# Another order of the eight head pairs in an encoder layer on one core, with two weight scans moved to other pairs

## The chip, the cores and the metric

One core of a Trainium2 chip. The metric is device time in microseconds (us) of one execution, and shorter is better. Five engines work side by side, each through its own queue in order: PE (matrix products), DVE (vector), ACT (activation functions), POOL and SP; SP here only issues transfers, the transposing ones among them. All dependencies between engines are semaphores.

## The reference, cut to what matters

One pre-norm layer over 2048 positions of width 1024. Eight heads of width 64 attend within a band of nine chunks of 64 positions (kind A); four heads of differential attention attend to everything up to the own chunk (kind B, two maps of width 64 for each head). Then an output projection, a gated FFN with a causal convolution, and norms.

```python
h = rmsnorm(x, attn_norm_g)
qa, ka, va, qb, kb, vb = jnp.split(h @ w_in, 6, axis=-1)
oa = chunked_band_attention(qa, ka, va, a_rel_bias)
ob = diff_attention(qb, kb, vb, t5_bias, lam, subln_g, lam_init)
x = x + jnp.concatenate([oa, ob], axis=-1) @ w_out
h = rmsnorm(x, ffn_norm_g)
u = causal_dwconv(h @ w_up, conv_w, conv_b)
gate, val = jnp.split(u, 2, axis=-1)
x = x + (jax.nn.silu(gate) * val) @ w_down
return rmsnorm(x, final_norm_g)
```

## The kernel before, in words

All products are made of float16 halves (a value is a high and a low part, three products of the four are added up). The attention works through eight head pairs, two heads of kind A (pairs 0 to 3) or the two maps of one kind B head (pairs 4 to 7), in the order of the list `ORDER` (L436). A place is a position in that list: place 1 is n = 0 in the code, place 8 is n = 7. Each pair has 16 blocks of 128 query rows.

For a block, `front_a` or `front_b` makes the scores on PE (L434, two PSUM banks for each piece of up to 512 keys), adds the bias and takes the maximum on DVE (L478 for A, L537 for B), forms the exponent's offset (L483, L541), takes the exponential on ACT (L486, L544), for B subtracts the second map from the first on DVE (L560; on ACT and POOL for some, L557 and L558), splits the result into halves (ACT L487 or L562, DVE and POOL L488, POOL L563) and has SP transpose it into the tile `pt` (L489, L565). Two blocks later `back_a` or `back_b` multiplies with the values (L509, L583). A block of kind A has rows of at most 640 keys, a block of kind B of up to 2048: A is the short kind, B the long one. Kind B goes through its blocks as 0, 15, 1, 14 and so on, kind A in order.

Between these steps, PE gets filler: `units(n)` lists the projections (L375) of the next pair's K, V and first Q, and of this pair's other Q, as generators; one pull is 6 products with 512 columns or 12 with 256. A pair takes 48 pulls, spread evenly over its 16 blocks, place 7 takes 32 and place 8 takes 28 over its first 11 blocks; after that place 8 pulls from the first output projection, `out_proj(0)` (L654). `beside(n)` holds what else is done at a block of a pair: the fetch of a weight slice and its row sums of squares (`scan_w`), its scaling and splitting (`load_w`, POOL and ACT), the bias of the next pair (`load_bias`). Two entries stand at place 7: `scan_wo` fetches w_out in eight pieces into two buffers (`wraw`) and squares them on ACT (L606), `scan_wd` fetches two pieces of w_down and takes their maxima on DVE (L614). Both results are needed only at place 8 or in the FFN.

Attention steps carry a high priority, and the framework's scheduler fixes each engine's order when the program is built; so the lists above set what can be chosen, and the printed order of each engine tells what came of it. Before the first pair, `make_profiles_b` writes the T5 profiles (31 small copies, L308) and `make_profiles` the band profiles, each to DRAM, from which `load_bias` reads rows. The FFN (L859 on) and the down product (L1258) follow in an order written out by hand.

Of the kernel before, what the change touches and what calls it, by code (L numbers as in the profile page):

```python
# [33 lines left out]
NH2 = 8  # L34
# [33 lines left out]
def kernel(  # L68
# [137 lines left out]
    with ExitStack() as at:  # L206
# [87 lines left out]
        def make_profiles():  # L294

            rr = sb.tile([8, 257], F32, name="rr", tag="PT", bufs=3)
            nc.gpsimd.dma_start(rr, rel_rev)
            pa = sb.tile([8, PROF], F32, name="pa", tag="HL", bufs=2)
            V.tensor_copy(pa[:, 0:127], rr[:, 0:1].to_broadcast([8, 127]))
            V.tensor_copy(pa[:, 127:PROF], rr[:, 0:256])  # L300
            nc.gpsimd.dma_start(prof[0:8], pa)

        def make_profiles_b():
            t5 = sb.tile([8, 32], F32, name="t5", tag="PT", bufs=3)
            nc.gpsimd.dma_start(t5, t5_t)
            pb = sb.tile([8, PROF], F32, name="pb", tag="HL", bufs=2)
            for j0, j1, k in T5_RUNS:
                V.tensor_copy(pb[:, j0:j1], t5[:, k:k + 1].to_broadcast([8, j1 - j0]))  # L308
            nc.gpsimd.dma_start(prof[8:16], pb)
# [123 lines left out]
                for hd, (a, b) in enumerate(((0, 64), (64, 128))):  # L433
                    nc.tensor.matmul(ps[hd], lhsT=qs[a:b, qa, qc], rhs=ks[a:b, ka, kc], start=n == 0, stop=n == 2)  # L434

        ORDER = [4, 5, 0, 6, 1, 7, 2, 3]  # L436
        oTl = {}

        def store_oT(c, tg, osb):
# [3 lines left out]
            V.tensor_tensor(hl[:, 1], src, hl[:, 0], ALU.subtract)  # L443
            last = c == ORDER[-1]
            st = kv.tile([P, 2, 4, P], F16, name="ost_l", tag="vs") if last else \
                sb.tile([P, 2, 4, P], F16, name="ost", bufs=1)
            nc.sync.dma_start_transpose(st.rearrange("p a t q -> p (a t) q"), hl.rearrange("p a b -> p (a b)"))
            if last:
                oTl[tg] = st
                return  # L450
            nc.sync.dma_start(oTd[tg, :, :, ORDER.index(c)], st)

# [181 lines left out]
        def out_proj(pc):  # L634


            for t in range(4):
                ss = tiny.tile([P, 2], F32, name="ss2")
                xs = []
                for sd in range(2):  # L640
# [9 lines left out]
                    for n in range(2):  # L650
                        k = 0
                        for c, oc in enumerate(lhs):
                            for a, b in TERMS:
                                nc.tensor.matmul(ps[n], lhsT=oc[:, a], rhs=wo[ORDER[c]][:, b, n * TG:(n + 1) * TG],  # L654
                                                 start=k == 0, stop=k == 3 * NC - 1)
# [51 lines left out]
        for tg in range(NG):  # L707
            make_h(tg, xts if tg == 0 else None)
            if tg == 0:
                for k, j in enumerate((2, 1, 0)):  # L710
                    scan_w(w, ORDER[0], j, raws[k] if k < len(raws) else None)
                    load_w(w, j, (True, KF, Q1)[k])
            proj_v_first(w, tg)
            run(proj_k(w, tg))
            if tg == 0:
                run(proj_q(w, 0))
                make_lambda()
                make_profiles_b()
                load_bias(w, ORDER[0])
        run(proj_q(w, 1))  # L720
        make_profiles()

        ws = [w] + [weights(n) for n in range(1, NH2)]
        first = out_proj(0)
# [16 lines left out]
        def beside(n):  # L741

            todo = {}
            if n == 0:
                todo[0, 0] = lambda: scan_w(ws[1], ORDER[1], 1)
                todo[0, 1] = lambda: load_w(ws[1], 1)
            if n + 1 < NH2:
                x = ws[n + 1]
                todo[3, 0] = lambda: scan_w(x, ORDER[n + 1], 2)
                todo[4, 1] = lambda: load_w(x, 2)  # L750
                todo[7, 0] = lambda: scan_w(x, ORDER[n + 1], 0)
                todo[8, 1] = lambda: (load_w(x, 0), load_bias(x, ORDER[n + 1]))
            if n + 2 < NH2:
                todo[13, 0] = lambda: scan_w(ws[n + 2], ORDER[n + 2], 1)
                todo[14, 1] = lambda: load_w(ws[n + 2], 1)
            if n == NH2 - 2:
                todo[10, 0] = scan_wo
                todo[13, 0] = scan_wd
            if n == NH2 - 1:
                todo[8, 1] = load_wo  # L760
            return todo
# [592 lines left out]
```

## Time and profile before

| | us |
|---|---|
| median of 3 runs | 2524.24 (2523.07 to 2527.94) |
| the profiled execution | 2528.28 |
| its span, first to last instruction | 2526.5 |
| busy PE / DVE / ACT / POOL in the span | 2379.4 / 1846.0 / 1354.3 / 1164.6 |
| first score product of place 1 | 79.5 |
| first score product of places 2 to 8 | 228.2, 376.6, 488.8, 640.8, 747.7, 896.8, 994.5 |
| first FFN product | 1273.6 |

The span holds a first part (norms, transposes and the first pair's projections), the attention, the output projection and the FFN. The starts of the places come from counting the score products (L434) in PE's order and taking the time of the first one of each pair from the trace. A stretch below is the time from one such start to the next one, and carries the number of its place. Granted clock 1.00 means that TensorE had its upper level (2.4 GHz) all through a stretch; 0.5 is the lower one (1.2 GHz).

### The profile page before, as it was taken

To read this page: it belongs to the slowest core of one execution; us is meant where nothing else is said; L and a number is where in the kernel's file an instruction comes from. 1 tells how busy PE (TensorE), PEld (TensorE's weight loads), DVE (VectorE), ACT (ScalarE), POOL (GpSimd) and SP (SyncE) were. 2 spreads that over 40 slices of the span, in tenths; PEclk is the share of its full clock that TensorE was granted. 3 is DMA by queue.
4 is the path that set the end of the run, shared out by engine and by line. 5 is a ranking of instruction groups with operands and counts; after the bars stand their busy time and mean duration, and the time that the engine had idled before them with its cause. 6 is when DMAs were issued, how large, how long until landed. Compare 5 with 4: busy or idle time off the path is not lost.

```text
span 2526.5 us, 42303 instructions
## 1 busy us (share of the span) xinstructions
PE 2379.4 (94%) x15382; PEld 1219.7 (48%) x15382; DVE 1846.0 (73%) x4359; ACT 1354.3 (54%) x2399; POOL 1164.6 (46%) x1127
## 2 busy tenths in 40 slices
PE   6999899999899988997978999999999999999998
PEld 5655555555565555543433444444444444444443
DVE  8678787568757885766566888888888776656555
ACT  7566566456655666644335666566556553333322
POOL 3343443234323332224234665666566464766654
PEclk9999899999999999998999999999999999999999
DMA  6154457635673579895995324333333339323322
GB/s 192 29 101 88 94 104 139 121 73 96 134 143 73 100 128 226 162 242 167 277 225 154 123 96 129 106 121 97 123 112 111 105 111 398 101 88 113 109 88 80
DMA packets 625378, 333.34 MB, mean 132 GB/s; under 512 B 447864, under 2 KB 592528, under 8 KB 623760
## 3 DMA queue, kind: packets, MB, share of 16 engines
q1 hardware_dynamic: 615264, 316.15, 50.2%
q0 software_dynamic: 2432, 8.42, 0.9%
q10 hardware_dynamic: 7472, 6.06, 0.8%
q8 instruction: 120, 1.97, 0.3%
q14 instruction: 90, 0.74, 0.1%
HBM read 145.73 MB, written 82.08 MB: 90 GB/s over the span
## 4 chain that ended last, share of the span: by engine, by line
PE 36%; DVE 6%; DMA 3%; ACT 3%; issue 2%; POOL 2%; SPq 1%; ACTq 0%; DVEq 0%; POOLq 0%
PE mm L859 21%; PE mm L1258 13%; DMA wd<-gd 2%; DVE Y L1058 1%; SPq L1093 1%; PE omm L654 1%; DVE wdhl L889 1%; ACT wuraw L959 1%; DMA T<-td 1%; DMA wdraw<-in_w_down_dram 0%; DMA wd<-wdd 0%; ACT Y L1062 0%; ACT wdhl L886 0%; DVE hl L681 0%; POOL wuhl L977 0%
## 5 line engine op out<-in xcount | busy, mean ns | idle before, releaser
L859 PE MATMUL mm<-T,wuhl 128*128 128x512 f16 x3696 | 809.0, 381 | 18.2 <-ACT tmp L1030 14.9
L859 PEld LDWEIGHTS <-wuhl 128*128 128x128 f16 x3696 | 363.4, 99 | 456.2 <-issue 25.5
L1258 PE MATMUL mm<-wd,ghl 128*128 128x512 f16 x1848 | 401.9, 380 | 4.7 <-ACT ghl L133 3.5
L375 PEld LDWEIGHTS <-whl 128*128 128x128 f16 x2976 | 273.1, 99 | 233.6 <-issue 81.4
L375 PE MATMUL mm<-h,whl 128*128 128x512 f16 x1440 | 349.2, 385 | 0.0
L434 PE MATMUL s<-ks,qs 64*128 64x256 f16 (+3 forms) x2160 | 282.1, 295 | 29.0 <-DVE mx L478 14.4
L1258 PEld LDWEIGHTS <-ghl 128*128 128x128 f16 x1848 | 180.7, 98 | 225.2 <-ACT ghl L133 4.8
L563 POOL TENSOR_TENSOR phl<-St,phl 128x1024 f16<-128x1024 f32 (+7 forms) x96 | 155.7, 1633 | 248.8 <-ACT phl L562 233.7
L1058 DVE SCALAR_TENSOR_TENSOR Y<-U,taps,Y 128x1024 f32<-128x1024 f32 x176 | 256.9, 1460 | 6.2 <-ACT Y L1054 4.6
L544 ACT ACTIVATE St<-St,nb,sc 128x1024 f32<-128x1024 f32 (+4 forms) x192 | 187.9, 979 | 50.3 <-DVE nb L541 50.3
L133 ACT ACTIVATE ghl<-wd,gsc 128x384 f16<-128x384 f32 (+1 forms) x176 | 106.6, 660 | 196.6 <-DMA wd<-gd 92.1
L134 DVE SCALAR_TENSOR_TENSOR ghl<-wd,gsc,ghl 128x384 f16<-128x384 f32 (+1 forms) x176 | 137.0, 812 | 94.3 <-ACT ghl L133 94.0
L375 PE MATMUL mq<-h,whl 128*128 128x256 f16 x1536 | 205.0, 278 | 0.0
L488 POOL TENSOR_TENSOR phl<-St,phl 128x640 f16<-128x640 f32 (+2 forms) x64 | 80.9, 1264 | 255.0 <-ACT phl L487 246.3
L434 PEld LDWEIGHTS <-qs 64*128 64x128 f16 x2160 | 114.4, 96 | 152.5 <-issue 108.0
L537 DVE CUSTOM_DVE_ANT_0 St<-s,near,mxb 128x512 f32<-128x512 f32 (+2 forms) x280 | 166.7, 620 | 25.5 <-PE s L434 19.8
L654 PE MATMUL omm<-wohl,oT 128*128 128x512 f16 x672 | 155.6, 386 | 18.5 <-DVE x L660 18.5
L889 DVE SCALAR_TENSOR_TENSOR wdhl<-wdraw,wd_sc,wdhl 128x128 f16<-128x128 f32 x132 | 141.5, 1087 | 30.8 <-ACT wdhl L886 29.7
L968 POOL TENSOR_TENSOR Sx<-wuraw 128x512 f32<-128x512 f32 x44 | 77.4, 1760 | 163.2 <-ACT wuraw L959 156.0
L1062 ACT ACTIVATE Y<-Y 128x1024 f32<-128x1024 f32 x44 | 46.5, 1057 | 182.2 <-DVE Y L1058 182.2
L486 ACT ACTIVATE St<-St,nb,sc 128x640 f32<-128x640 f32 (+4 forms) x128 | 107.9, 843 | 59.3 <-DVE nb L483 58.1
L562 ACT ACTIVATE phl<-St 128x1024 f16<-128x1024 f32 (+7 forms) x96 | 75.6, 802 | 114.1 <-DMA pt<-phl 56.6
(229 smaller groups left out, 3765.9 us busy)
## 6 DMA issues: line engine op xcount, KB each, us to landing
wd<-gd SPq DMA_DIRECT2D x88, 256.0 KB, 2.8
wuraw<-in_w_up_dram SPq DMA_DIRECT2D x42, 512.0 KB, 5.2
gd<-Y SPq DMA_DIRECT2D x42, 512.0 KB, 2.8
wdraw<-in_w_down_dram SPq DMA_DIRECT2D x154, 128.0 KB, 2.8
wd<-wdd SPq DMA_DIRECT2D x11, 1792.0 KB, 13.1
wdd<-wdhl SPq DMA_DIRECT2D x41, 448.0 KB, 2.7
wraw<-in_w_in_dram SPq DMA_DIRECT2D x24, 512.0 KB, 3.9
td<-hl SPq DMA_DIRECT2D x24, 512.0 KB, 5.0
```

Of the source, the lines that this page charges most:

```text
L134: V.scalar_tensor_tensor(lo, src, scale, hi, ALU.mult, ALU.subtract)
L375: nc.tensor.matmul(ps, lhsT=hl[:, a, c, :], rhs=h[:, b, c, t0:t1], start=n == 0, stop=n == 3 * NC - 1)
L434: nc.tensor.matmul(ps[hd], lhsT=qs[a:b, qa, qc], rhs=ks[a:b, ka, kc], start=n == 0, stop=n == 2)
L486: A.activation(St, St, AF.Exp, bias=nb[:, hd:hd + 1], scale=w["sc"], accum_out=l[:, hd:hd + 1])
L537: V.tensor_tensor_reduce(Sm[hd][g][:, a0:a0 + b - a], ps[hd][:, :b - a], bias, 1.0, m[hd], ALU.add, ALU.max, mx[:, hd, f:f + 1])
L544: A.activation(Sm[hd][g], Sm[hd][g], AF.Exp, bias=nb[:, hd:hd + 1], scale=w["sc"], accum_out=l[:, hd, g:g + 1])
L563: nc.gpsimd.tensor_tensor(hl[:, 1], Sm[0][g], hl[:, 0], ALU.subtract)
L654: nc.tensor.matmul(ps[n], lhsT=oc[:, a], rhs=wo[ORDER[c]][:, b, n * TG:(n + 1) * TG], start=k == 0, stop=k == 3 * NC - 1)
L859: nc.tensor.matmul(ps, lhsT=hl[:, a, wop, c * P:(c + 1) * P], rhs=Tt[:, b, c, :], start=start and k == 0, stop=k == 11, skip_group_check=n ...
L889: V.scalar_tensor_tensor(dst, src, scale, h, ALU.mult, ALU.subtract)
L1058: V.scalar_tensor_tensor(Y, self.U[j][:, tap:D + tap], self.u.taps[j][:, tap:tap + 1], Y, ALU.mult, ALU.add)
L1258: nc.tensor.matmul(ps[m].rearrange("p (c n) -> p c n", c=4), lhsT=g[kb][:, a, go], rhs=wd[kb][:, :, c_, wo_], start=kb == k0 and k == 0, s ...
```

## The change

The list of pairs becomes 0, 4, 1, 5, 2, 6, 7, 3. In letters, before B B A B A B A A, now A B A B A B B A. Place 8 keeps pair 3. Since a pair of kind A comes first, its profiles are written ahead of the T5 ones. `scan_wo` moves from place 7 to place 4 (a pair of kind B), `scan_wd` from place 7 to place 6 (also B). The pulls stay with the places: 48, and 32 and 28 at the last two.

```diff
--- before.py
+++ after.py
@@ -433,7 +433,7 @@
                 for hd, (a, b) in enumerate(((0, 64), (64, 128))):
                     nc.tensor.matmul(ps[hd], lhsT=qs[a:b, qa, qc], rhs=ks[a:b, ka, kc], start=n == 0, stop=n == 2)
 
-        ORDER = [4, 5, 0, 6, 1, 7, 2, 3]
+        ORDER = [0, 4, 1, 5, 2, 6, 7, 3]
         oTl = {}
 
         def store_oT(c, tg, osb):
@@ -715,10 +715,10 @@
             if tg == 0:
                 run(proj_q(w, 0))
                 make_lambda()
-                make_profiles_b()
+                make_profiles()
                 load_bias(w, ORDER[0])
         run(proj_q(w, 1))
-        make_profiles()
+        make_profiles_b()
 
         ws = [w] + [weights(n) for n in range(1, NH2)]
         first = out_proj(0)
@@ -753,9 +753,10 @@
             if n + 2 < NH2:
                 todo[13, 0] = lambda: scan_w(ws[n + 2], ORDER[n + 2], 1)
                 todo[14, 1] = lambda: load_w(ws[n + 2], 1)
-            if n == NH2 - 2:
+            if n == 3:
                 todo[10, 0] = scan_wo
-                todo[13, 0] = scan_wd
+            if n == 5:
+                todo[10, 0] = scan_wd
             if n == NH2 - 1:
                 todo[8, 1] = load_wo
             return todo
```

What the scheduler makes of it at two places.

PE at place 7, where the weights of the next pair's query slice are summed (`am`). Before, the pair of kind A; `o` is the product with the values, `mm` and `mq` are filler:

```order
L375 LDWEIGHTS whl
L375 MATMUL mm<-h,whl 128x512
L152 MATMUL am<-ws_ss,ones 128x1
L509 LDWEIGHTS pt
L509 MATMUL o<-vs,pt 128x64
```

Now, the pair of kind B, the same point (`s` are scores):

```order
L375 LDWEIGHTS whl
L375 MATMUL mm<-h,whl 128x512
L152 MATMUL am<-ws_ss,ones 128x1
L434 LDWEIGHTS qs
L434 MATMUL s<-ks,qs 128x256
```

In the first piece, 30 products with the values follow the sum, and then filler again. In the second, 93 score products and 150 products with the values follow it before the next filler product: a run of 243 products without filler, for which the order of before has no counterpart.

SP's queue around `scan_wo`. Before, at place 7 (`pt` are the transposed probabilities, `ost` and `oTd` the output of four blocks):

```order
L605 DMA woraw<-in_w_out_dram 128x1024
L489 DMA_TRANSPOSE pt<-phl 128x20x128
L447 DMA_TRANSPOSE ost<-ohl 128x8x128
L489 DMA_TRANSPOSE pt<-phl 128x20x128
L451 DMA oTd<-ost 256x1x512
L489 DMA_TRANSPOSE pt<-phl 128x20x128
L605 DMA woraw<-in_w_out_dram 128x1024
L397 DMA_TRANSPOSE vs<-vt 128x8x128
L605 DMA woraw<-in_w_out_dram 128x1024
```

Now, at place 4:

```order
L605 DMA woraw<-in_w_out_dram 128x1024
L352 DMA rows<-prof 128x2x256
L605 DMA woraw<-in_w_out_dram 128x1024 x3
L565 DMA_TRANSPOSE pt<-phl 128x16x128
L565 DMA_TRANSPOSE pt<-phl 128x10x128
L605 DMA woraw<-in_w_out_dram 128x1024 x2
L447 DMA_TRANSPOSE ost<-ohl 128x8x128
L565 DMA_TRANSPOSE pt<-phl 128x10x128
```

The eight fetches stand closer together, three of them in a row ahead of two transposes, and each fetch from the third on waits for a square on ACT to give a buffer back.

## Rows read from the trace of the kernel before

**Rows 1.** The page: busy time of each engine in the span.
```profile
span 2526.5 us, 42303 instructions
PE 2379.4 (94%) x15382; PEld 1219.7 (48%) x15382; DVE 1846.0 (73%) x4359; ACT 1354.3 (54%) x2399; POOL 1164.6 (46%) x1127
```

**Rows 2.** Stretches 1 to 8: busy us of each engine, granted clock, DMA share, GB/s.
```profile
core 0: us, PE busy (x) PEld busy (x) DVE busy (x) ACT busy (x) POOL busy (x), PEclk, DMA share, GB/s
79.50:228.20 148.70, 141.54 (x1171) 82.66 (x1171) 109.59 (x362) 87.72 (x177) 57.86 (x33) 0.98 0.43 83
228.20:376.60 148.40, 136.00 (x1078) 76.02 (x1076) 122.38 (x396) 86.93 (x181) 59.46 (x34) 0.94 0.49 90
376.60:488.80 112.20, 108.12 (x1034) 64.52 (x1033) 71.57 (x258) 65.69 (x140) 34.53 (x23) 0.97 0.74 135
488.80:640.80 152.00, 144.66 (x1146) 79.06 (x1145) 115.60 (x365) 88.96 (x179) 57.61 (x34) 0.98 0.49 91
640.80:747.70 106.90, 100.53 (x1010) 61.40 (x1008) 75.02 (x257) 63.01 (x134) 33.93 (x23) 0.95 0.68 131
747.70:896.80 149.10, 141.88 (x1147) 78.15 (x1145) 115.38 (x367) 89.33 (x179) 57.38 (x33) 1.00 0.51 97
896.80:994.50 97.70, 85.56 (x909) 53.24 (x909) 68.84 (x243) 65.14 (x138) 31.04 (x21) 0.95 0.89 176
994.50:1273.60 279.10, 250.60 (x1761) 128.37 (x1756) 183.05 (x413) 137.72 (x225) 79.72 (x60) 0.94 0.86 210
```

**Rows 3.** Waits of PE in stretch 2: us in total, times, longest.
```profile
PE s L434 <- DVE mxb L537: 6.6, 7, 3.0
PE o L583 <- DMA pt<-phl: 5.7, 3, 3.3
```

**Rows 4.** Groups by line of PE in stretch 2, the filler: count | busy us, mean ns.
```profile
L375 PE MATMUL mm<-h,whl 128*128 128x512 f16 x192 | 45.9, 380 | 0.0
L375 PE MATMUL mq<-h,whl 128*128 128x256 f16 x181 | 26.5, 283 | 0.0
```

**Rows 5.** Groups by line of DVE, stretches 1 to 7: count | busy us, mean ns.
```profile
L134 DVE SCALAR_TENSOR_TENSOR qs<-mq,qs 128x256 f16<-128x256 f32 x56 | 23.1, 413 | 12.9 <-ACT qs L133 12.7
L134 DVE SCALAR_TENSOR_TENSOR ks<-mm,ks 128x512 f16<-128x512 f32 x27 | 18.5, 684 | 17.1 <-ACT ks L133 17.0
L560 DVE SCALAR_TENSOR_TENSOR St<-St,ratio 128x256 f32<-128x256 f32 x4 | 7.7, 1920 | 0.1
L560 DVE SCALAR_TENSOR_TENSOR St<-St,ratio 128x512 f32<-128x512 f32 x4 | 3.0, 749 | 0.1
L614 DVE TENSOR_REDUCE wd_m<-wdfirst 128x1 f32<-128x1024 f32 x2 | 2.4, 1220 | 1.1 <-DMA wdfirst<-in_w_down_dram 1.1
```

**Rows 6.** Short windows of the attention, columns as in Rows 2.
```profile
900.00:950.00 50.00, 42.76 (x476) 26.94 (x474) 42.06 (x151) 34.41 (x81) 17.35 (x13) 1.00 0.75 139
330.00:340.00 10.00, 9.15 (x63) 4.24 (x61) 9.72 (x24) 4.82 (x11) 5.63 (x3) 1.00 0.56 68
```

**Rows 7.** The tile woraw: instructions, ns min/median/max, first and last start us.
```profile
L605 SPq DMA_DIRECT2D woraw<-in_w_out_dram x8: 333/592/1177, 931.2 to 982.2; - x8
L606 ACT ACTIVATE woraw<-woraw x8: 1040/1052/1058, 938.2 to 987.8; 128x1024 f32<-128x1024 f32 x8
...
  ACT woraw L606: 7.2, 4
```

**Rows 8.** Waits of PE in stretch 7 and, last row, in the output projection.
```profile
PE s L434 <- DVE mx L478: 4.9, 5, 2.8
PE o L509 <- DMA pt<-phl: 4.0, 1, 4.0
...
PE omm L654 <- DVE x L660: 18.5, 2, 13.5
```

**Rows 9.** The T5 copies, and the first part's busy time (columns as in Rows 2).
```profile
L308 DVE COPY pb<-t x31: 131/147/235, 6.0 to 8.5; 8x1 f32<-8x1 f32 x15, 8x4 f32<-8x4 f32 x4, 8x27 f32<-8x27 f32 x2, 8x18 f32<-8x18 f32 x2
...
0.00:79.50 79.50, 58.97 (x559) 47.41 (x560) 65.81 (x284) 51.71 (x90) 27.02 (x25) 0.98 0.51 153
```

**Rows 10.** The page, costliest groups: POOL's subtraction for kind B.
```profile
L563 POOL TENSOR_TENSOR phl<-St,phl 128x1024 f16<-128x1024 f32 (+7 forms) x96 | 155.7, 1633 | 248.8 <-ACT phl L562 233.7
```

**Rows 11.** The line L560: instruction, count, ns min/median/max, first and last start us.
```profile
L560 DVE SCALAR_TENSOR_TENSOR St<-St,ratio x80: 344/1274/3049, 83.0 to 902.6; 128x1024 f32<-128x1024 f32 x36, 128x128 f32<-128x128 f32 x8, 128x896 f32<-128x896 f32 x8, 128x384 f32<-128x384 f32 x8
```

## The prediction, made before the changed kernel ran

> **What bounds the kernel now.** I read the page first, then a table by stretch, then the waits of single stretches. The page says PE: it is busy for 94% of the span, DVE for 73% [rows 1]. That is an average, so the table cuts the attention where one pair's scores give way to the next pair's [rows 2]. There PE is busy for 136 to 145 us of each long stretch of about 150, and for 86 to 108 us of a short one; ACT and POOL are far below, while DVE has 109.6 to 122.4 us of work in a long stretch and about 70 to 75 in a short one. So PE sets the pace, DVE is second, and the balance differs by kind: a long pair brings some 40 us more DVE work than a short one.
>
> What can be won or lost by an order is what PE loses. I define the **loss** of a stretch as its length minus PE's busy time at full clock (busy time multiplied by the granted clock). From [rows 2], stretch 1: 148.7 - 141.54 x 0.98 = 10.0. In the same way stretches 2 to 7 lose 20.6, 7.3, 10.2, 11.4, 7.2 and 16.4. The sum is 83.1 us. Two stand out. Stretch 2 is a long pair that follows a long pair; its waits are for DVE's maxima (6.6 us, which hold back the next scores) and for transposed probabilities (5.7 us) [rows 3], and its mean granted clock was 0.94, so PE worked part of it at its lower level. DVE was busy for 122.38 of 148.4 us there, 82.5%, the highest share of the eight. Stretch 7 is a short pair with only 32 pulls of filler, with the scans of w_out and w_down beside it and a DMA share of 0.89; its waits are of the same two kinds [rows 8].
>
> **The change part by part.** All products stay, so PE's work at full clock is the same in total; only the losses change. The new sequence has three short pairs (places 1, 3, 5), three long pairs behind a short one (2, 4, 6), and a long pair behind a long one at place 7, with 32 pulls. Place 8 keeps its pair and its 28 pulls.
>
> *Short pairs.* Two short stretches with 48 pulls are on record, with losses of 7.3 and 11.4: I take 9.4 each, 28.1 for three (21.9 to 34.2). No row shows a short pair at place 1. The long pair there loses 10.0, no less than a short one later on, so nothing asks for another value.
>
> *Long pairs behind a short one.* 10.2 and 7.2 are on record: I take 8.7 each, 26.1 for three (21.6 to 30.6).
>
> *The long pair at place 7*, the term that decides. Its nearest row is stretch 2, the other long pair behind a long one. Against it, the printed order of the changed kernel has 96 instead of 192 filler products with 512 columns and 207 instead of 181 with 256. At the busy time for each of these in stretch 2, 45.9 / 192 = 0.239 and 26.5 / 181 = 0.146 us [rows 4], that is 22.9 us less and 3.8 more: PE is left with 116.9 us, or 109.9 at full clock. DVE loses far less. The 96 products are 4 projections with one DVE eviction each, 0.684 us; the 26 others are one more, 0.413 us [rows 5]; so 122.4 - 2.7 + 0.4 = 120.1 us. **Here DVE has 10 us more work than PE**, which holds for no other long stretch, and the order shows where: a run of 243 products without filler, in which every score waits for a bank that DVE has to empty. How densely can DVE be packed? 82.5% is the most over a stretch, 42.06 of 50 us, 84.1%, the most that I found over 50 us, and 97% was reached over 10 us [rows 6]. With 82.5% the stretch takes 145.6 us, with 84.1% it takes 142.8, with 97% it would take 123.8. I take the middle of the first two, 144.2, since they are the longest averages; the loss is then 144.2 - 109.9 = 34.3 (13.9 to 35.7).
>
> *The scan of w_out.* Eight squares of 1.05 us on ACT and eight fetches through SP [rows 7]. Place 4 has room for both: ACT is busy for 59% of stretch 4 against 67% of stretch 7, and the DMA share is 0.49 against 0.89. But SP's queue now has three fetches in a row ahead of two transposes, each fetch waiting for a square, and PE's products with the values wait for such transposes. The upper bound is what stretch 7 loses beyond a short pair with 48 pulls, 16.4 - 9.4 = 7.0, all of it laid on the scan; the lower bound is 0, not a gain, because the long stretches that I take for place 4 have no scan. I take 2, near the lower end, as the long pair is the roomier place.
>
> *Edits with one answer.* The scan of w_down is two reductions of 1.22 us on DVE [rows 5] and two fetches; at place 6 they lie in the 34 us in which DVE is idle, and uncovered they would cost 2.4. The T5 copies (31 of some 0.15 us, done at 8.5 us before) [rows 9] move behind the band profiles; in the printed order both still stand ahead of the first block, some 70 us after the copies were done before. Zero, and at most 4.6 if nothing covered them. Place 8 keeps its work; the order of two DVE evictions of the output projection changes near the spot where PE waited 13.5 us [rows 8], so I leave the loss of stretch 8 as it is and give it 5 us either way in the range.
>
> *Sum.* 28.1 + 26.1 + 34.3 + 2 = 90.5 against 83.1: **7.4 us slower**. The profiled execution would go from 2528.28 to 2535.7; it lay 4.0 above the median of the runs shown, so the median goes from 2524.24 to 2531.6, and I give 2531.5.
>
> **A rule set against the rows.** The four subtractions of 256 columns on L560 took 1.920 us on average, the four of 512 columns 0.749 [rows 5]; size does not do that, and the surplus is about one POOL subtraction, 1.633 us [rows 10]. The Trainium skill, SBUF — State Buffer, section on SBUF's two separate sides, says that a DVE instruction with two SBUF inputs and a GpSimd instruction exclude each other for a whole instruction; the trace agrees. By the rule alone each of the 20 subtractions of a long pair (80 in four pairs [rows 11]) could wait that long at place 7: an estimate of 32.7 us more DVE work, a stretch of at least 152.8 us, a loss of 42.9 and a sum 16.0 above before, 2540.2. The rows of stretch 2 have what such meetings cost inside their 122.4 us, so my sum stays with them, and this rival gets 0.02. By that rule a denser place 7 would have more such meetings, not fewer, which speaks against the second rival below.
>
> **The rivals.** *No measurable change.* (A measurement of this kernel can tell about 0.2%, 5 us, from nothing.) The sum is even when place 7 loses 26.9, a stretch of 136.8 us, DVE at 87.8%. Between 84.7% and 91.1% the time stays within 5 us of before. For it: single windows are denser than that. Against: no 50 us are. About 2524.
>
> *Faster: place 7 stays paced by PE.* The mechanism is the backlog: the scores of two blocks are issued ahead, the first and last thirds of the pair still have filler, and only the run without it waits, with PE's other 32-pull stretch as a model. Stretch 7 lost 16.4 with a scan in it, so a long one could lose about as little. It decides from a DVE share of 91.1% on; at the 97% of the densest window the loss is 13.9, and 28.1 + 26.1 + 13.9 + 2 = 70.1 is 13.0 us less than before: 2511. For it: removing the pair-behind-pair at place 2 is a sure gain of some 12 us (20.6 against 8.7). Against: DVE would need 97% over 124 us.
>
> *Slower by more: the scan blocks SP at place 4.* The three fetches hold two transposes back, and the whole upper bound of 7.0 falls due instead of 2: 2536.5. For it: ACT waited 7.2 us for these fetches before [rows 7]. Against: the same queue was as crowded at place 7.
>
> That the change does not do what it says can be excluded by the printed order: pairs and scans stand where the list puts them.
>
> **How the numbers follow.** DVE-paced place 7: 0.42, of which 0.06 ends inside 0.2%. DVE stretched by POOL: 0.02. No change: 0.22. PE-paced: 0.28. The scan: 0.06. So slower by over 0.2% 0.44, within it 0.28, faster 0.28. The forecast's own range takes the scan from 0 to 7.0, the other losses and stretch 8 at their bounds: 2526 to 2543. With the PE-paced case at 2511 the range is 2511 to 2543; left out are the ends where several bounds fall together.
>
> **What would show it.** Right: stretch 7 takes about 144 us, DVE above 82% in it and PE below 82%, with waits for L537 well over 6.6 us; stretch 2 loses about 9 instead of 20.6. Wrong: a stretch 7 below 137 us; a stretch 4 well over 152; or a loss at place 1 unlike 9. If the sum of the losses comes out as worked and the time does not, the cause lies in stretch 8 or behind it.

## The result, and the profile after

The changed kernel takes 2555.43 us (median of 4 runs, 2552.6 to 2558.78) against 2523.65 for the kernel before in the same comparison: a ratio of 1.0123, 95% interval 1.0107 to 1.014. It is 31.8 us slower; 7.4 were forecast, and the time lies 12 us above the range.

The page of the changed kernel, the busy times [rows 1] and the score products:

```profile
span 2554.5 us, 42320 instructions
PE 2400.4 (94%) x15382; PEld 1227.2 (48%) x15382; DVE 1851.4 (72%) x4359; ACT 1356.3 (53%) x2399; POOL 1166.8 (46%) x1127
...
L434 PE MATMUL s<-ks,qs 64*128 64x256 f16 (+3 forms) x2160 | 294.0, 295 | 46.1 <-DVE mxb L537 32.3
```

The same group on the page of the kernel before:

```profile
L434 PE MATMUL s<-ks,qs 64*128 64x256 f16 (+3 forms) x2160 | 282.1, 295 | 29.0 <-DVE mx L478 14.4
```

The same 15382 products keep PE "busy" for 21.0 us longer (2400.4 against 2379.4), 11.9 of it on the score products, whose number and shapes are the same. That is the first thing that the prediction did not allow for. The table by stretch, first part ahead, columns as in [rows 2]:

```profile
0.00:83.60 83.60, 60.31 (x558) 48.60 (x558) 65.96 (x286) 50.84 (x90) 26.35 (x25) 0.98 0.46 145
83.60:201.20 117.60, 113.86 (x1068) 68.83 (x1067) 66.27 (x229) 61.79 (x125) 32.84 (x22) 0.96 0.56 104
201.20:354.50 153.30, 147.76 (x1149) 80.41 (x1146) 115.75 (x367) 89.21 (x179) 57.40 (x34) 0.96 0.48 94
354.50:460.20 105.70, 97.60 (x1009) 59.99 (x1008) 72.63 (x255) 63.25 (x134) 34.09 (x23) 0.98 0.73 131
460.20:613.00 152.80, 143.98 (x1088) 75.80 (x1086) 113.58 (x362) 94.02 (x189) 57.58 (x33) 0.97 0.57 116
613.00:724.00 111.00, 103.86 (x1069) 65.17 (x1067) 76.34 (x259) 66.30 (x139) 36.36 (x24) 0.98 0.69 135
724.00:882.70 158.70, 147.78 (x1152) 80.11 (x1150) 118.37 (x366) 89.33 (x179) 58.45 (x34) 0.96 0.51 97
882.70:1023.90 141.20, 125.76 (x1006) 73.90 (x1004) 120.86 (x393) 82.71 (x175) 54.58 (x32) 0.92 0.49 93
1023.90:1303.60 279.70, 247.98 (x1714) 125.43 (x1713) 186.69 (x425) 139.37 (x231) 82.67 (x62) 0.96 0.85 206
```

The prediction's loss (length minus busy time multiplied by the clock) comes to 8.3, 11.4, 10.1, 13.1, 9.2, 16.8 and 25.5 for stretches 1 to 7: 94.4, against 83.1 before and 90.5 forecast. Stretch 8 loses 41.6 (43.5 before). The whole difference between the two profiled executions splits so (the clock has two digits, so the second and third lines can each be off by one or two us):

| us | before | changed | difference |
|---|---|---|---|
| first part, to the first score product | 79.5 | 83.6 | +4.1 |
| stretches 1 to 8: loss | 126.6 | 136.1 | +9.5 |
| stretches 1 to 8: PE busy time multiplied by the clock | 1067.5 | 1083.9 | +16.4 |
| first FFN product to the end | 1254.7 | 1252.7 | -2.0 |
| the profiled execution | 2528.28 | 2556.26 | +28.0 |

The third line is the largest, and by the prediction it should have been zero. This is the split of one build; other builds of the same list split otherwise, as the section on why the prediction was wrong shows. What the third line holds here shows in PE's timeline at the border from place 1 (short) to place 2 (long). Columns: start, duration, instruction, count.

```profile
213.54 0.51 PE L509 MATMUL o<-vs,pt 128*128 128x64 f16 x12
213.98 0.39 PE L434 MATMUL s<-ks,qs 64*128 64x512 f16 x1
214.30 0.20 PE L509 MATMUL o<-vs,pt 128*128 128x64 f16 x1
214.44 0.39 PE L434 MATMUL s<-ks,qs 64*128 64x512 f16 x1
214.75 0.20 PE L509 MATMUL o<-vs,pt 128*128 128x64 f16 x1
...
219.26 0.61 PE L434 MATMUL s<-ks,qs 64*128 64x512 f16 x1
219.80 0.56 PE L509 MATMUL o<-vs,pt 128*128 128x64 f16 x7
220.17 1.47 PE L375 MATMUL mq<-h,whl 128*128 128x256 f16 x6
```

A score product and a value product alternate twelve times. No wait stands between them, yet one step of two products takes 0.455 us (213.98 to 214.44, 214.44 to 214.89). The 30 value products and 12 scores take 6.63 us together, from 213.54 to 220.17, all of it counted as busy. The last steps are longer than the first ones (from start to start, a score takes 0.54 us at 219.26 and 0.32 at 213.98), since the granted clock had fallen by then.

The windows over this border, columns as in [rows 2]:

```profile
211.00:234.00 23.00, 23.00 (x128) 10.11 (x127) 11.74 (x45) 8.91 (x22) 0.43 (x1) 0.78 0.18 39
213.00:219.00 6.00, 6.00 (x40) 2.86 (x37) 3.19 (x10) 0.58 (x2) 0.43 (x1) 0.95 0.12 24
219.00:229.00 10.00, 10.00 (x44) 4.06 (x43) 3.97 (x14) 6.54 (x13) 0.00 (x0) 0.52 0.14 26
```

PE shows no idle time in them, and still the granted clock falls to its lower level (0.52 from 219 to 229 us) at the end of the alternation.

### The profile page after: what moved, and what is told of

The parts are those of the page before. It is cut to its first block, busy times and chain, and to the rows that moved or that the text cites. A ratio compares the mean times of both kernels' runs of the same rounds, so it can differ in the third digit from the quotient of the medians.

```text
span 2554.5 us, 42320 instructions
## 1 busy us (share of the span) xinstructions
PE 2400.4 (94%) x15382; PEld 1227.2 (48%) x15382; DVE 1851.4 (72%) x4359; ACT 1356.3 (53%) x2399; POOL 1166.8 (46%) x1127
## 4 chain that ended last, share of the span: by engine, by line
PE 40%; DMA 4%; DVE 3%; SPq 3%; POOL 1%; ACT 1%; issue 1%; ACTq 0%; DVEq 0%; POOLq 0%
PE mm L860 27%; PE mm L1259 13%; SPq L1094 2%; DMA wd<-gd 2%; DMA T<-td 1%; DVE Y L1059 1%; DMA x1k<-in_x_dram 0%; DMA wd<-wdd 0%; ACT wuraw L960 0%; DVE wdhl L890 0%; POOL wd L1236 0%; DMA wdraw<-in_w_down_dram 0%; DVE T L674 0%; POOL wd L1239 0%; DMA td<-hl 0%
## 5 line engine op out<-in xcount | busy, mean ns | idle before, releaser
L375 PE MATMUL mm<-h,whl 128*128 128x512 f16 x1440 | 355.8, 389 | 0.0
L434 PE MATMUL s<-ks,qs 64*128 64x256 f16 (+3 forms) x2160 | 294.0, 295 | 46.1 <-DVE mxb L537 32.3
L537 DVE CUSTOM_DVE_ANT_0 St<-s,near,mxb 128x512 f32<-128x512 f32 (+3 forms) x280 | 167.2, 622 | 23.3 <-PE s L434 19.6
L654 PE MATMUL omm<-wohl,oT 128*128 128x512 f16 x672 | 156.9, 387 | 22.5 <-DVE x L660 16.7
```

Source lines behind the costliest of these rows:

```text
L375: nc.tensor.matmul(ps, lhsT=hl[:, a, c, :], rhs=h[:, b, c, t0:t1], start=n == 0, stop=n == 3 * NC - 1)
L537: V.tensor_tensor_reduce(Sm[hd][g][:, a0:a0 + b - a], ps[hd][:, :b - a], bias, 1.0, m[hd], ALU.add, ALU.max, mx[:, hd, f:f + 1])
```

## The experiments

Three suspects stood at first: the scans in their new places, the front of the sequence (a short pair at place 1 instead of a long one), and its back (a long pair behind a long one at place 7). A fourth came from the timeline: value products mixed with scores. The letters that an expectation uses for theories are its own; "HA" below is the offset of the high priority (1000) that all attention steps share. Percentages are against the kernel before on the same chip.

**The scans alone.** The order of before, with the scans at places 4 and 6.

```diff
-            if n == NH2 - 2:
+            if n == 3:
                 todo[10, 0] = scan_wo
-                todo[13, 0] = scan_wd
+            if n == 5:
+                todo[10, 0] = scan_wd
```

> The kernel before with its own order of pairs; only the two scans are moved, w_out's to place 4 (pair 6, long) and w_down's to place 6 (pair 7, long). Theory 1 (the long pair at place 7, with 32 pulls of filler, costs most of the 31.8 us): moving the scans alone costs 0 to 7 us, and may gain a few since place 7 gets rid of them; 2519 to 2531. Theory 2 (the scans cost most: stretches 4 and 6 of the changed kernel are the ones that grew beside stretch 7): 10 to 18 us slower, 2534 to 2542. Theory 3 (the short pair at place 1 costs): 2519 to 2527, no change.

1.0027 (1.0014 to 1.0041), 2537.76 against 2530.18. By the ratio that is 6.8 us slower for both scans together, near the upper bound of 7.0 that the prediction gave the scan of w_out, not the 2 that it took. It lies at the upper end of theory 1.

**The order alone.** The changed kernel with both scans back at place 7.

```diff
-            if n == 3:
+            if n == NH2 - 2:
                 todo[10, 0] = scan_wo
-            if n == 5:
-                todo[10, 0] = scan_wd
+                todo[13, 0] = scan_wd
```

> The changed kernel with the two scans put back to place 7, so only the order of pairs (and of the profiles) is changed. Theory 1: the long pair at place 7 still costs, and now has the scans as well: 2550 to 2565. Theory 2: what the scans cost at places 4 and 6 comes back: 2536 to 2546. Theory 3: the start's 4 us stay, 2550 to 2556.

1.0119 (1.0088 to 1.015). The interval holds the changed kernel's 1.0123: in the new order the scans' place cannot be told from nothing, and the order carries the loss. Whether the costs of the two edits add up cannot be told: 0.27% and 1.19% against 1.23%, with intervals that allow it.

**Long first, then in turn.** Scans at place 7, list `[4, 0, 5, 1, 6, 2, 7, 3]`: long pairs at places 1, 3, 5, 7, each behind a short one or first.

```diff
-        ORDER = [4, 5, 0, 6, 1, 7, 2, 3]
+        ORDER = [4, 0, 5, 1, 6, 2, 7, 3]
```

> The kernel before with long and short pairs in turn from a long one on (4, 0, 5, 1, 6, 2, 7, 3): long at place 1, no two long pairs in a row, a long pair at place 7 with 32 pulls; the scans stay at place 7. Theory 1: the long pair at place 7 costs here too, 15 us or more with the scans beside it: 2538 to 2555. Theory 2: no scan is moved, so no more than 5 us from before: 2519 to 2529. Theory 3: no short pair first, so the start is as before: 2519 to 2529.

1.0024 (1.0009 to 1.0039). A long pair at place 7 by itself costs little: with the scans beside it, it took 136.7 us there.

**A short pair first, and no long one at place 7.** `[0, 4, 5, 1, 6, 7, 2, 3]`, scans at place 7, T5 copies last as in the changed kernel.

```diff
-        ORDER = [4, 5, 0, 6, 1, 7, 2, 3]
+        ORDER = [0, 4, 5, 1, 6, 7, 2, 3]
```

> Short pair first, short pair at place 7, the scans at place 7 (0, 4, 5, 1, 6, 7, 2, 3): against the kernel before, only the start of the list differs in kind, with two times two long pairs in a row. Theory 1: the place 7 is short again, so within 5 us of before but for the second row of long pairs (a loss of about 12 more there): 2520 to 2537. Theory 2: no scan is moved: 2519 to 2532. Theory 3 (the short first pair costs by itself, 4 us in the first part and more behind): 2530 or above.

1.0154 (1.0135 to 1.0172), the slowest of all. So the long pair at place 7 is not needed for the loss: a short start together with two long pairs in a row, at places 2 and 3 and again at 5 and 6, does it too. The run does not part these two.

**Places 1 and 2 exchanged.** The changed kernel with a long pair first again, and the T5 profiles first (the second edit is not shown).

```diff
-        ORDER = [0, 4, 1, 5, 2, 6, 7, 3]
+        ORDER = [4, 0, 1, 5, 2, 6, 7, 3]
```

> The changed kernel with places 1 and 2 exchanged (4, 0, 1, 5, 2, 6, 7, 3), so a long pair comes first again; the two long pairs at places 6 and 7, the 32 pulls and both moved scans stay as in the changed kernel. Theory A (a long pair is cheap at place 1, where nothing of a pair before it lies between its scores, and dear at every later place): 15 to 25 us of the 31 come back, 0.2% to 0.6% above before. Theory B (the time goes at places 6 and 7 and with the scans): no more than 5 us come back, 1.0% to 1.3% above before.

1.0089 (1.0068 to 1.0109), 2550.53. By the ratios, 8.6 us of the 31 come back; neither theory is met as stated. The front would be about a quarter, at the edge of the noise: the two intervals touch (1.0107 and 1.0109).

**Both sets of profiles ahead of the first bias.** The changed kernel with `make_profiles_b()` directly behind `make_profiles()`.

```diff
                 make_lambda()
                 make_profiles()
+                make_profiles_b()
                 load_bias(w, ORDER[0])
         run(proj_q(w, 1))
-        make_profiles_b()
```

> The changed kernel with both sets of profiles written ahead of the first pair's bias. Theory C (the 4 us of the first part come from the T5 copies, which now stand between the norms' steps on DVE): the first score product comes at 79 to 80 us again instead of 83.6, and the whole is 4 us shorter, 1.1% above before. Rival (the 4 us come from the short pair's own start or from the order that the scheduler found): first score at 83 to 86 us, no change in the whole.

1.0107 (1.0081 to 1.0134). The interval overlaps with the changed kernel's, so no gain in the time is shown. The first score product, however, comes at 80.7 us instead of 83.6. Over all profiles, it came at 83.6 to 86.3 in the five where the T5 copies stand behind the first bias, and at 79.3 to 81.9 in all others. In the two pairs of kernels that differ in this alone it is 2.9 us (83.6 to 80.7) and 4.6 us (86.1 to 81.5, in the last experiment). So the copies' place costs the first part about 3 to 5 us.

**The scans at short pairs.** The order of before, scans at places 3 and 5 (n == 2 and n == 4), both short.

```diff
-            if n == NH2 - 2:
+            if n == 2:
                 todo[10, 0] = scan_wo
-                todo[13, 0] = scan_wd
+            if n == 4:
+                todo[10, 0] = scan_wd
```

> The kernel before with its own order; the scans at short pairs with full filler, w_out's at place 3 (pair 0), w_down's at place 5 (pair 1). At long pairs they cost: stretches 4 and 6 grew by some 8 us each in loss, stretch 7 gave 5 back, 0.27% in all. If what they cost is DVE's and ACT's lack of room in a long pair: stretches 3 and 5 grow by 3 us at most and stretch 7 gives 5 back, so 2 to 5 us faster than before, 0.1% to 0.2%. If they cost wherever they are put (the order of SP and of the buffers): same as before to 7 us slower.

1.0068 (1.0049 to 1.0087). That is 17 us slower, more than either expectation had it, and slower than with the scans at long pairs. PE's printed order shows that moving a scan regroups the products: scores that stand alone between two value products are 105 before and 128 here.

**Full filler at place 7.** The changed kernel with all of the K and V projections of place 8 pulled at place 7 (48 pulls, 12 at place 8). The lists in `units` change with it and are not shown.

```diff
-        CHUNKS = {NH2 - 2: 32, NH2 - 1: 28}
+        CHUNKS = {NH2 - 2: 48, NH2 - 1: 12}
```

> The changed kernel with the projections of place 8 all pulled at place 7: 48 pulls there and 12 at place 8 instead of 32 and 28. If the lack of filler is what place 7 loses (DVE 10 us over PE): the loss of stretch 7 falls from 36 to about 24 us against products at their start-to-start time, the whole is 8 to 12 us shorter, 0.8% above before, unless place 8 loses it again. If a long pair behind a long one loses that much anyway: stretch 7 grows by the 21 us of products moved into it, stretch 8 shrinks by as much, and the whole stays within 5 us, 1.1% to 1.4% above before.

1.0124 (1.0101 to 1.0147): no net gain. Its stretches 7 and 8:

```profile
885.60:1038.80 153.20, 139.88 (x1082) 77.09 (x1081) 122.61 (x388) 84.94 (x178) 53.13 (x32) 0.93 0.49 91
1038.80:1309.90 271.10, 237.60 (x1640) 121.65 (x1637) 183.91 (x430) 137.87 (x228) 81.93 (x61) 0.92 0.86 208
```

Stretch 7 loses 153.2 - 139.88 x 0.93 = 23.1 instead of 25.5, but stretch 8 loses 52.5 instead of 41.6. The filler taken from place 8 is missed there.

**Value products ahead of the scores.** Now the fourth suspect. The two pulls of value products between pieces of scores get a higher priority than the scores, so the scheduler puts each block's value products out in one piece. One line in `attention`:

```diff
-                        with tc.high_priority(offset=HA):
+                        with tc.high_priority(offset=1030):
                             pull(back, 2)
```

On the order of before, with nothing else changed:

> The kernel before; only the priority of the products with the values is raised a little above that of the scores, so that where both are ready PE's order takes the values in one piece instead of one value product and one score product in turn. Changes between score products (64 rows) and others fall from 896 to 634 in the printed order. Theory D (each change costs PE about 0.096 us, and the alternating runs at the border from a short to a long pair bring the clock down as well): 25 us from the changes and some 10 from the clock, 2490 to 2510 where before is 2525. Rival (the time at the border is DVE's or the clock's own and comes back elsewhere): within 5 us of before, or slower since a block's scores come later.

0.995 (0.9932 to 0.9968), 2515.4 against 2528.12. It is faster than both kernels, and by 13 us than the one before: more than the rival's 5, far less than the 35 of theory D.

On the changed order:

> The changed kernel with the same edit; 928 changes fall to 656. Theory D: 26 us from the changes, 10 to 15 from the clock at three borders, so its distance to the kernel before with the same edit shrinks from 31 to 15 to 22 us (what is left is the run without filler at place 7, the two long pairs in a row and the T5 copies). Rival (the border has nothing to do with the difference): the distance stays at 28 to 34 us.

0.9984 (0.9968 to 1.0), 2521.98. The two orders, 31.8 us apart, are 6.6 us apart in the medians of these two runs (8.6 by the ratios), closer than either expectation had it. On the order `[4, 0, 5, 1, 6, 2, 7, 3]`:

> The order 4, 0, 5, 1, 6, 2, 7, 3 (scans at place 7, as in the kernel before) with the same edit. Without it this order was 0.24% above before, with three borders from short to long against two. Theory D: the third border costs less now, so it lands within 3 us of the kernel before with the edit, or below it. Rival: 0.2% to 0.4% above it.

0.9976 (0.9962 to 0.999), 2522.29. That is 0.26% above the order of before with the same edit, as the rival had it and not theory D: between these two orders the distance (0.24% without the edit) has not shrunk. In all three no score stands alone any more between value products. The score products and PE on the page of the order of before with values ahead:

```profile
PE 2343.3 (93%) x15382; PEld 1208.7 (48%) x15382; DVE 1847.3 (73%) x4359; ACT 1356.0 (54%) x2399; POOL 1162.7 (46%) x1127
...
L434 PE MATMUL s<-ks,qs 64*128 64x256 f16 (+3 forms) x2160 | 248.9, 294 | 36.1 <-DVE mxb L537 18.6
```

and of the changed order with values ahead:

```profile
PE 2343.2 (93%) x15382; PEld 1208.2 (48%) x15382; DVE 1851.1 (74%) x4359; ACT 1355.1 (54%) x2399; POOL 1166.3 (46%) x1127
...
L434 PE MATMUL s<-ks,qs 64*128 64x256 f16 (+3 forms) x2160 | 249.3, 291 | 45.7 <-DVE mxb L537 27.5
```

282.1 and 294.0 us for the scores have become 248.9 and 249.3. The same border in the timeline of the changed order with values ahead, and a later piece of it:

```profile
207.81 1.05 PE L509 MATMUL o<-vs,pt 128*128 128x64 f16 x30 [0.71 <-DMA pt<-phl]
208.79 1.50 PE L434 MATMUL s<-ks,qs 64*128 64x512 f16 x12
210.22 1.16 PE L375 MATMUL mq<-h,whl 128*128 128x256 f16 x9
...
220.75 0.83 PE L434 MATMUL s<-ks,qs 64*128 64x512 f16 x6
221.51 1.47 PE L375 MATMUL mm<-h,whl 128*128 128x512 f16 x6
```

30 value products and 12 scores of 512 columns take 2.41 us here (207.81 to 210.22), after a wait of 0.71; in the changed kernel they took 6.63. Six scores in a row, three for each head, take 0.76 us (220.75 to 221.51). Three in a row, of one head, take the same, as the kernel before shows (237.37 to 238.12):

```profile
237.37 0.82 PE L434 MATMUL s<-ks,qs 64*128 64x512 f16 x3
238.12 0.28 PE L375 MATMUL mq<-h,whl 128*128 128x256 f16 x1
```

So the 64-row products of the two heads run side by side, but only while they follow each other. The Trainium skill, TensorEngine Tiling (Array Packing), section Key Properties, says that tiles can compute in parallel and that changing the tiling mode drains TensorE; the intervals agree with both. They also give the size, which it does not: from one start to the next, in the trace of the changed kernel, a filler product of 512 columns takes 0.216 us before another one and 0.312 before a score; a value product of 64 columns takes 0.029 before another and 0.136 before a score; and a score of 512 columns takes 0.216 before another of the same head and 0.308 before a product of another kind. A change costs about 0.1 us either way.

**Values behind the scores.** The same line with an offset of 200, on the order of before.

```diff
-                        with tc.high_priority(offset=HA):
+                        with tc.high_priority(offset=200):
                             pull(back, 2)
```

> The kernel before; the priority of the products with the values is lowered well below that of the scores. The printed order then has no score product that stands alone between two value products (105 before), but more changes between score products and others: 946 against 896. Theory D1 (what costs is the one-by-one run, by its changes and by the clock that falls in it): a gain, but smaller than with the values ahead, since the changes stay: 2515 to 2525 where before is 2528. Theory D2 (each change costs 0.096 us and nothing else matters): 5 us slower, 2530 to 2536. Rival: the values come later and PE waits for banks: slower by more than 5 us.

1.0109 (1.0071 to 1.0147), 26 us slower in the medians. Neither theory is borne out as stated; the rival's range holds. No score stands alone here either, yet the scores take 311.4 us:

```profile
L434 PE MATMUL s<-ks,qs 64*128 64x256 f16 (+3 forms) x2160 | 311.4, 294 | 47.4 <-DVE mx L478 28.0
```

PE's printed order has 313 runs of exactly three scores, that is of one head; before there are 157. The waits of the scores grow too, 47.4 us against 29.0.

**More mixing.** The same line with offset 970 on the order of before: 280 scores alone between value products (105 before), 1258 changes between scores and other products (896 before), and 156 runs of three.

> The kernel before; the priority of the value products is set 30 steps below that of the scores, where the two mix most: 1258 changes (896 before) and 280 score products alone between two value products (105 before). Theory D: 362 more changes at 0.096 us are 35 us, and more falls of the clock; 2560 to 2590 where before is 2528. Rival (the mixed order costs nothing by itself, PE having time between waits): within 10 us of before.

1.0097 (1.0065 to 1.0129), 24 us slower where 35 or more were expected.

```profile
PE 2421.0 (95%) x15382; PEld 1237.5 (49%) x15382; DVE 1837.4 (72%) x4359; ACT 1361.6 (54%) x2399; POOL 1172.7 (46%) x1127
...
L434 PE MATMUL s<-ks,qs 64*128 64x256 f16 (+3 forms) x2160 | 317.5, 295 | 21.1 <-DVE mx L478 12.4
```

PE is busy for 41.6 us more than before, and the idle time ahead of the scores falls from 29.0 to 21.1: part of what mixing costs is taken out of waits that PE would have had anyway.

**Values ahead and both profiles ahead**, on the changed order.

> The changed kernel with the values ahead of the scores and with both sets of profiles written ahead of the first pair's bias. What is left between the two kernels with the values ahead is 8.6 us by their ratios; in the profile, the first score product came 6.8 us later than in the one with the old order. If that start is the rest of the difference: 4 to 7 us less than without the edit, 0.990 to 0.9965 of before. If the run without filler at place 7 is the rest: 0.997 to 1.000 of before, as without the edit.

0.9976 (0.9955 to 0.9997). The first score product comes at 81.5 us instead of 86.1, but the interval overlaps with that of the run without the move (0.9968 to 1.0). What the first part's gain is worth in the whole stays open.

## Why the prediction was wrong

**The step that failed is "All products stay, so PE's work at full clock is the same in total; only the losses change."** The products stay, but their order on PE doesn't, and in the changed kernel busy time multiplied by the clock grew by 16.4 us, the largest part of the 20.6 us that the profiled execution took beyond the forecast. With values ahead the same sum over stretches 1 to 8 is 1029.4 us in the order of before and 1039.4 in the changed one: 38.1 and 44.5 us less than without. This time lay inside what I took for work.

The printed orders tell where it arises. Scores alone between value products at places 1 to 8 are 5, 5, 28, 24, 11, 24, 8, 0 before and 25, 24, 11, 22, 6, 26, 9, 3 after. A long pair behind a short one brings 22 to 26, a long pair at place 1 or behind it only 5, and a short pair at place 1 brings 25, as the first short pair of before, at place 3, brings 28. The runs of three are 157 and 164. From the intervals above, a mixed step takes 0.455 us where an unmixed score and value product take 1.43 / 12 + 0.98 / 30 = 0.152, so a score alone costs 0.30 us; a run of three costs half of 0.75, 0.37 us. For 21 more and 7 more that is 6.4 + 2.6 = 9.0 of the 16.4 us. These prices are estimates from scores of 512 columns. The remaining 7 are not settled: also with values ahead the changed order has 10.0 us more in this line, and 3.5 more in the last experiment, where only the T5 copies stand elsewhere.

How much of that can be won back differs by order. With values ahead the work falls by 38.1 us in the order of before, but its losses rise from 126.6 to 153.3, so 11.4 are left. In the changed order 44.5 fall, the losses rise by 2.2 (136.1 to 138.3), and 42.3 are left. That is why the two orders end close together. That the changed order simply had fewer waits to hide the mixing in is my reading; no experiment showed it by itself.

**How far this account reaches.** It is read from the one build that the prediction was about. The same sums for four of the experiments limit it (differences to the kernel before in us, as in the table of the result):

| | ratio | first part | loss | busy time multiplied by the clock |
|---|---|---|---|---|
| the changed kernel | 1.0123 | +4.1 | +9.5 | +16.4 |
| the order alone | 1.0119 | +4.2 | +41.5 | -3.6 |
| both profiles ahead | 1.0107 | +1.2 | +17.2 | +8.2 |
| places 1 and 2 exchanged | 1.0089 | +1.4 | +22.1 | +1.0 |
| short first, short at place 7 | 1.0154 | +6.7 | +41.2 | +1.4 |

The first three have the same list of pairs and are slower by about the same share. With the scans back at place 7, however, all of it lies in the losses, most at places 6 and 7, where the granted clock was low (26.7 and 36.0 us of loss):

```profile
727.20:890.40 163.20, 150.03 (x1121) 81.67 (x1122) 116.22 (x359) 88.61 (x177) 58.27 (x33) 0.91 0.47 88
890.40:1035.20 144.80, 123.61 (x1030) 75.36 (x1027) 124.77 (x395) 91.35 (x191) 55.85 (x31) 0.88 0.61 127
```

(The profiled executions of the second and the last row were each the longest of four, so part of their loss may be the clock of that execution alone.) And with places 1 and 2 exchanged PE's order is no more mixed than before (860 changes against 896, 106 scores alone against 105, 139 runs of three against 157), yet the kernel is 0.89% slower. So mixing, counted in this way, does not explain the whole price of these orders. What the experiments show is that the price of the changed order hangs on how value products and scores are put together: with the values in one piece, 31.8 us become 6.6. Without that edit the time appears as busy time in one build and as waits and clock in another; what decides between them stays open.

**Point by point.**

- *Short pairs*, 28.1 forecast: 8.3 + 10.1 + 9.2 = 27.6. Right as a loss, at place 1 too. The mixing at place 1 (25 scores alone) lies outside the loss; the first short pair of before, at place 3, has 28.
- *Long pairs behind a short one*, 26.1 forecast: 11.4 + 13.1 + 16.8 = 41.3, above the upper bound of 30.6. This term of the sum failed too, by 15.2 us. Their stretches take 152.8 to 158.7 us, where the two of before took 152.0 and 149.1 [rows 2]. About half of the 15.2 us is the clock. PE is busy all through the windows that hold the alternations at these borders, so what the clock takes there is their length times what is missing from 1.00. At 211 us that is 23 x 0.22 = 5.1; the other two of the changed kernel, then the two of before:

```profile
472.00:487.00 15.00, 15.00 (x88) 6.97 (x85) 7.40 (x25) 6.40 (x13) 0.43 (x1) 0.77 0.14 27
736.00:753.00 17.00, 17.00 (x91) 7.36 (x89) 8.03 (x29) 7.84 (x18) 0.43 (x1) 0.70 0.16 37
...
501.00:516.00 15.00, 15.00 (x87) 6.65 (x84) 7.32 (x25) 6.98 (x14) 0.43 (x1) 0.77 0.13 26
760.00:775.00 15.00, 15.00 (x99) 6.82 (x98) 8.85 (x35) 7.54 (x17) 0.41 (x1) 1.00 0.21 48
```

That is 13.6 us at three borders, where the forecast, with three times the mean of the two of before (3.5 and 0), had 5.2. With the values in one piece the same three borders of the changed order were granted 1.00:

```profile
196.60:240.00 43.40, 41.67 (x363) 22.63 (x361) 29.65 (x99) 27.73 (x55) 12.34 (x9) 1.00 0.47 90
445.80:490.00 44.20, 41.97 (x359) 22.43 (x358) 29.64 (x98) 27.15 (x55) 11.97 (x9) 1.00 0.50 89
699.00:745.00 46.00, 42.91 (x373) 23.49 (x370) 30.59 (x102) 28.14 (x55) 13.06 (x9) 1.00 0.47 86
```

- *Long pair at place 7*, 34.3 forecast: 25.5. The stretch takes 141.2 us (144.2 forecast) with 120.86 us of DVE work (120.1), and DVE is busy for 85.6% of it, a little above the 84.1% of [rows 6]. The mechanism is borne out in part: PE's longest waits are the scores' for DVE's maxima, 13.4 us, as in stretch 2 before [rows 3] and longer. But PE was busy for 89% of the stretch, where the prediction wanted below 82%, and some 10 of the 25.5 us are the clock (0.92), not waits. Nor was 84.1% the most over 50 us: in the kernel before, DVE was busy for 91% from 574 to 624 us, so the argument against the rival of no measurable change, that no 50 us are denser, was wrong. The waits of PE in stretch 7 of the changed kernel (total, times, longest):

```profile
PE s L434 <- DVE mxb L537: 13.4, 15, 3.6
PE o L583 <- DMA pt<-phl: 1.2, 2, 0.8
```

The 50 us of the kernel before, columns as in [rows 2]:

```profile
574.00:624.00 50.00, 46.53 (x377) 25.90 (x378) 45.52 (x137) 28.40 (x59) 17.81 (x12) 1.00 0.58 105
```

The rival in which POOL stretches DVE's work by 32.7 us is excluded by the 120.86.
- *The scan of w_out*, 2 forecast: 6.8 us in the order of before, with the scan of w_down moved too, and nothing that can be told from zero in the changed one.
- *The T5 copies*, 0 forecast: the first part is 4.1 us longer, and 2.9 of it goes when the copies go ahead again.
- *Stretch 8*, unchanged forecast: 41.6 against 43.5. The output projection's wait, 18.5 before [rows 8], is 16.7.

By its own quantity, the loss, the sum was near in this build: +11.3 for stretches 1 to 7 against +7.4. That was luck: place 7 and the long pairs behind short ones were off in opposite directions, and with the order alone the same seven stretches came to +40.6. The sentence that was to catch a failure ("the cause lies in stretch 8 or behind it") was itself wrong: most of the difference lay in the same stretches, in the busy time.

The Trainium skill, Perfetto Trace Analysis, section Identifying the Most-Contended Engine, says that the busy share of matmul is no good measure of how near a kernel is to the limit. These runs agree: 15382 products were busy for 2343.2 to 2421.0 us in the kernels of this document, by their order and the clock that they were granted.

## What to carry to other kernels

When a change reorders work on the bounding engine, compare the time from start to start of equal products, not only idle time: "busy" may hold drains. Before reordering units, count in the printed order how often neighbouring products change shape, and how often products that can run side by side are split up; here one priority that keeps value products in one piece gained more (0.5%) than any order of the pairs that was tried. The count is a warning and no forecast: the exchanged order has no higher count than the kernel before and is 0.89% slower. Nor is one build the measure of an order: the same list split its loss otherwise with the scans elsewhere. A cost read from a unit in one place (long behind short, 8.7 us) holds only for the same neighbours and mixing, so read each new neighbour's border on PE too.

## What the runs showed of the hardware that was not expected

- A change between 64-row and 128-row products costs about 0.1 us in both directions (into a score 0.216 to 0.312 and 0.029 to 0.136, out of a score 0.216 to 0.308, from start to start), and is counted as busy.
- Three scores of 512 columns for one head take 0.75 us, six for two heads 0.76.
- The granted clock fell to 0.52 from 219 to 229 us while PE showed 10.00 us busy of 10.00. Before it fell, PE had alternated scores and value products for 4.4 us. This is no single case: the traces of these kernels hold 28 such alternations of twelve steps or more (3 in the changed kernel, 2 in the one before, 23 in the experiments), and in 25 of them the granted clock falls inside the alternation or within 0.3 us of its end. With the values in one piece there is no such alternation, and the three borders of the changed order were granted 1.00, as shown above.
- Other falls have no alternation ahead of them: with the values in one piece, stretch 7 of the changed order was granted 0.90. How the alternation leads to the lower level stays open.
